# FFN up-projection as seven products per block pair (Strassen), with the second token half's norm behind products of the first

## The chip, the core and the metric

The kernel runs on one core of a Trainium2 chip. Its engines run beside one another, each through its own instructions in order: TensorE (PE) multiplies, and its weight loads (PEld) overlap its matmuls; VectorE (DVE), ScalarE (ACT) and GpSimd (POOL) work on elements; SyncE (SP) issues the transfers (DMAs). The metric is the device time of one execution in microseconds, the median of three runs.

## What is computed

One decoder layer over 16 meta tokens and 1024 tokens of width 1024, all in float32: retention and differential attention side by side, merged by gates, then a gated MLP with a causal convolution of three taps. Cut to the parts that the change touches:

```
do  = do @ w_diff_o                                   # 1024 x 1024
mix = (sigmoid(g_ret) * ro + sigmoid(g_diff) * do) @ w_out
h   = h + mix
u   = rmsnorm(h, norm2_w)
up  = causal_dwconv(u @ w_up, conv_w, conv_b)         # 1024 -> 2 x 2816
a, b = split(up)
h   = h + (silu(a) * b) @ w_down                      # 2816 -> 1024
```

## The kernel before

Activations lie transposed: channels on the 128 partitions in blocks, tokens along the columns. A float32 product is made of three matmuls of a shorter type: each operand is split into a high and a low part, and hi x hi, hi x lo and lo x hi are summed in PSUM. For weights this split is two instructions per [128, 4, 128] half block: ACT casts the high part (L227), POOL subtracts it from the raw weight for the low part (L230). The matmuls of all bulk products stand in one helper (L175).

The program runs through five stages. Phase 1 and phase 2 (projections, differential attention, retention and its output product, lines 942 and before) end near 1657 us. Phase 3 scales the eight attention heads (L971, split at L247), multiplies them by `w_diff_o` and merges them with the gates (L991 to L998), multiplies the result by `w_out` and adds it to the residual (`finish`, L1019), with the squares for the norm gathered on ACT and POOL (L1022 to L1026). Phase 4 is the FFN: for each of 22 blocks f of 128 hidden channels, `up(f)` and `up(22 + f)` multiply eight blocks of the input by one weight block over three token groups of 342 (two halo columns and 1024 tokens), so 8 x 3 x 3 = 72 matmuls. The input is h times the norm weight; the factor of the token, 1/rms, is multiplied onto the finished product (L1079), so that the products needn't wait for the norm. Then come the three taps of the convolution on DVE (`conv`, L1086 and L1088), Silu on ACT (L1124), the product with the other half (L1125), its split (ACT and POOL at L247), and for two blocks at a time the down product, 48 matmuls of 512 columns per block, added into h by DVE (L1103).

What sets the order: one list of weight blocks through the whole program (`self.stream`, `next_w`) keeps two blocks loaded and split ahead, from any stage into the next. Work for other engines that PE would wait for is put off by units of twelve matmuls (`defer`, `tick`). All tiles come from pools that live for the whole program.

## Time and profile before

| | us |
|---|---|
| median of three runs | 2614.26 (2612.69 to 2614.82) |
| profiled execution, first to last instruction (span) | 2609.7 |
| PE busy | 2520.9 (97%), 15444 matmuls |
| DVE busy | 1667.5 (64%) |
| ACT busy | 898.4 (34%) |
| POOL busy | 865.4 (33%) |

What lies outside the span of the profiled execution is the start and the end of the program, 4.6 us between the span and the median. A busy share is an average over the stages. What counts for a change in one stage is the table by windows: there each engine's busy time stands for one stretch, beside the clock that was granted to PE. A group of instructions gives the mean time of one; how close they follow one another is read from the starts in the timeline. The DMA queues of the page hold loads and stores that SP issues; none is issued from POOL.

### The profile page before, as it was taken

The numbers are of one execution on the slowest core, as the hardware profiler recorded it, in microseconds if no ns is written. First come the engines' busy times: TensorE is split into PE (matmuls) and PEld (weight loads), VectorE is DVE, ScalarE is ACT, GpSimd is POOL, SyncE is SP. The second block draws the span as 40 slices with busy tenths as digits, with TensorE's granted clock in tenths as the row PEclk, the third lists the DMA queues.
The fourth block names the chain that finished last, engine by engine and source line by source line (L and its number), as shares of the span: only waits on it lengthen the run. The fifth ranks groups of instructions, "written<-read, shape, count | busy, mean of one in ns | idle before, by whom it ended". The sixth has DMA issues, their size and how long they took to land.

```text
span 2609.7 us, 40439 instructions
## 1 busy us (share of the span) xinstructions
PE 2520.9 (97%) x15444; PEld 2420.4 (93%) x15444; DVE 1667.5 (64%) x3359; ACT 898.4 (34%) x1903; POOL 865.4 (33%) x644
## 2 busy tenths in 40 slices
PE   7899999999999999999999999999999999999999
PEld 6898999999999999999999898999999999999998
DVE  8687877657474756654677888452376555555555
ACT  3344434344252433433456654332321111111111
POOL 4433343313132222212333333443333333333332
PEclk8999999999999999999999999999999999999999
DMA  4121221222222121223343434523111111111112
GB/s 175 58 78 64 67 79 61 81 87 67 84 64 78 57 87 62 75 83 103 108 115 86 120 88 122 177 98 112 45 48 47 49 49 49 43 47 49 49 49 85
DMA packets 165777, 205.37 MB, mean 79 GB/s; under 512 B 25560, under 2 KB 108112, under 8 KB 165584
## 3 DMA queue, kind: packets, MB, share of 16 engines
q1 hardware_dynamic: 165440, 202.70, 24.4%
q8 instruction: 121, 1.98, 0.3%
q14 instruction: 72, 0.59, 0.1%
q10 hardware_dynamic: 144, 0.10, 0.0%
HBM read 160.20 MB, written 42.35 MB: 78 GB/s over the span
## 4 chain that ended last, share of the span: by engine, by line
PE 76%; DVE 15%; issue 4%; ACT 2%; DMA 2%; SPq 1%; POOL 0%; DVEq 0%; ACTq 0%; POOLq 0%
PE acc L175 43%; PE sc L175 27%; PE ot L175 3%; DVE b L567 3%; PE st L175 2%; DMA b<-d 1%; DVE b L499 1%; ACT b L609 1%; PE sc L625 1%; DVE b L602 1%; DVE al L247 1%; DVE b L501 1%; DVE sql L247 1%; DVE sh L498 1%; DVE b L521 1%
## 5 line engine op out<-in xcount | busy, mean ns | idle before, releaser
L175 PE MATMUL acc<-b,wh 128*128 128x342 f32 (+3 forms) x6076 | 1484.6, 327 | 30.7 <-DVE b L252 6.6
L175 PEld LDWEIGHTS acc<-b,wh 128*128 128x128 f32 x6076 | 1055.1, 190 | 46.3 <-DVE b L253 7.3
L175 PE MATMUL acc<-b,wl 128*128 128x342 f32 (+3 forms) x3038 | 987.2, 325 | 0.3 <-POOL wl L230 0.3
L230 POOL TENSOR_TENSOR wl<-wr,wh 128x512 fp32r<-128x512 f32 x370 | 514.1, 1408 | 1114.2 <-ACT wh L227 1103.8
L175 PE MATMUL sc<-b,wh 128*128 128x342 f32 (+2 forms) x2452 | 616.2, 334 | 0.0
L175 PEld LDWEIGHTS acc<-b,wl 128*128 128x128 f32 x3038 | 577.0, 190 | 5.7 <-POOL wl L230 0.6
L175 PEld LDWEIGHTS sc<-b,wh 128*128 128x128 f32 x2452 | 432.1, 189 | 20.9
L227 ACT CAST wh<-wr 128x512 fp32r<-128x512 f32 x370 | 214.6, 618 | 574.2 <-issue 286.3
L175 PE MATMUL sc<-b,wl 128*128 128x342 f32 (+2 forms) x1226 | 410.6, 335 | 0.8 <-POOL wl L230 0.8
L247 POOL TENSOR_TENSOR b<-b,b 128x512 fp32r<-128x512 f32 (+2 forms) x90 | 147.9, 1644 | 317.2 <-ACT b L242 275.4
L175 PEld LDWEIGHTS sc<-b,wl 128*128 128x128 f32 x1226 | 231.8, 189 | 11.4 <-POOL wl L230 1.3
L242 ACT CAST b<-b 128x512 fp32r<-128x512 f32 (+2 forms) x135 | 99.9, 745 | 233.0 <-DVE b L1125 146.2
L609 ACT ACTIVATE b<-b,sm 128x272 f32<-128x272 f32 (+7 forms) x128 | 100.9, 789 | 227.0 <-DVE sm L608 174.6
L534 DVE TENSOR_TENSOR ev<-acc,b 128x342 f32<-128x342 f32 (+1 forms) x144 | 74.0, 514 | 132.8 <-PE acc L175 115.8
L1088 DVE SCALAR_TENSOR_TENSOR b<-b,cols,b 128x1024 f32<-128x1024 f32 x88 | 148.8, 1691 | 2.3
L602 DVE CUSTOM_DVE_ANT_0 b<-sc,consts 128x144 f32<-128x144 f32 (+6 forms) x224 | 105.9, 503 | 42.7 <-PE sc L175 42.1
L1079 DVE TENSOR_TENSOR b<-sc,b 128x342 f32<-128x342 f32 x84 | 42.5, 511 | 137.3 <-PE sc L175 137.3
L247 DVE TENSOR_TENSOR al<-sc,ah 128x512 fp32r<-128x512 f32 (+2 forms) x144 | 77.5, 539 | 56.8 <-ACT ah L242 55.4
L1103 DVE TENSOR_TENSOR b<-b,sc 128x512 f32<-128x512 f32 x117 | 78.6, 682 | 48.9 <-PE sc L175 48.9
L242 ACT CAST ah<-sc 128x512 fp32r<-128x512 f32 (+2 forms) x144 | 67.3, 468 | 122.3 <-PE sc L625 94.5
L500 POOL TENSOR_TENSOR sh<-sh,b 128x346 f32<-128x346 f32 (+1 forms) x48 | 47.7, 994 | 153.4 <-DVE sh L498 125.5
L567 DVE TENSOR_TENSOR b<-b,b 64x346 fp32r<-64x346 f32 (+1 forms) x96 | 89.4, 931 | 3.7 <-ACT b L566 0.7
(230 smaller groups left out, 2849.6 us busy)
## 6 DMA issues: line engine op xcount, KB each, us to landing
wr<-w_in SPq DMA_DIRECT2D x176, 256.0 KB
wr<-w_up SPq DMA_DIRECT2D x88, 256.0 KB
d<-ev SPq DMA_DIRECT2D x120, 171.0 KB
b<-d SPq DMA_DIRECT2D x256, 64.0 KB
b<-d SPq DMA_DIRECT2D x24, 513.0 KB
wr<-w_down SPq DMA_DIRECT2D x44, 256.0 KB
b<-d SPq DMA_DIRECT2D x32, 260.0 KB
d<-ev SPq DMA_DIRECT2D x48, 173.0 KB
```

Of the source, the lines that this page charges most:

```text
L175: self.E.matmul(out, lhsT=l, rhs=r, start=start, stop=stop)
L227: self.A.copy(h, raw)
L230: self.G.tensor_sub(l, raw, h.bitcast(F32))
L242: self.A.copy(dh, src)
L247: (self.V if el == "V" else self.G).tensor_sub(dl, src, dh.bitcast(F32))
L500: G.tensor_mul(sh[:, :n], sh[:, :n], self.Sn[:, cs])
L534: V.tensor_mul(o[:, :n], ps[:, :n], self.rb[:, cs])
L567: V.tensor_sub(dst[o, cs], raw[r, cs], dst[r, cs].bitcast(F32))
L602: V.tensor_tensor_reduce(out=sc_[:m, a0:a0 + sz], in0=ps[:m, :sz], in1=mk, scale=1.0, scalar=3e38, op0=ALU.add, op1=ALU.min, accum_out=sm[ ...
L609: A.activation(sc_[:m, :n], sc_[:m, :n], AF.Exp, bias=mx, scale=-1.0, accum_out=sm[:m, 10 + c:11 + c])
L1088: V.scalar_tensor_tensor(out=o[:, q], in0=up[:, NMETA - 2 + i:T - 2 + i], scalar=self.cw(i, fi), in1=o[:, q], op0=ALU.mult, op1=ALU.add)
L1103: self.V.tensor_add(h, h, ps)
```

## The change

**The up-projection.** For a pair of weight blocks (f and 22 + f), the input channels are cut in two halves, the tokens in two halves of 516 columns (two pieces of 258), and the two blocks are the two halves of the output. That is a 2 x 2 matrix product, and it is made with seven products instead of eight, by Strassen's algorithm in Winograd's form. The products are named A, B, D, E, F, G, H. A and B use plain quarters of the input; E, F, G, H use sums and differences of its quarters, made once (`operand_e` to `operand_h`); each product has 4 x 3 x 2 = 24 matmuls of 258 columns. Their weights are sums of quarters too, made for each pair: two of the sums by DMAs that add what they load to what lies in SBUF, issued from POOL (`quad_sums`, L1291 and L1292), two by POOL (`weights`, names S and T, L1303 and L1305); every weight quarter is then cast by ACT and split by POOL (L983). B, H, G and D are accumulated onto the bank of an earlier product after DVE or ACT has read that bank, so that a bank holds running sums. DVE has five reads of PSUM per pair (L1417, L1427, L1434, L1439, L1442), ACT two. The first tap of the convolution goes from DVE to ACT (`Identity` with a scale and a bias); the other two are on DVE as before, in halves of 512 columns (L1340), put between the reads of the next pair, the product with the other half too (L1356).

**Norm.** Sums of halves of the tokens need inputs with the norm's factor in them. So h is multiplied by 1/rms and the norm weight before the products (`scaled`, L1238). w_out is done in two token halves, and its weights are loaded twice; the norm of the first half runs during the second half's products, that of the second half behind the products A and B of the first three pairs, which need the first half alone.

**Order.** The pools of phases 1 and 2 are closed and others opened (`back`), with their own weight queue, quarter tiles (11 for high and low parts, 8 raw) and PSUM layout; the last two blocks of `w_ret_o` are moved behind that border. Head norms are put between the products of the merge, one at a time (`normed_head`). The results of all 22 pairs are stored to DRAM, and all down products come after the last pair, with the same number of matmuls as before; h waits in DRAM meanwhile.

```diff
+    def back(self, ctx):
...
+        self.flush()
+        self.front.close()
+        tc, a = self.tc, self.a
+        pool = lambda n, b=1, **k: ctx.enter_context(tc.tile_pool(name=n, bufs=b, **k))
+        self.tp = pool("tmp2", 1)
+        self.wp = pool("w2", 11)
+        self.ps = pool("ps2", 3, space=PSUM)
+        self.queue = [a["w_ret_o"][14], a["w_ret_o"][15]] + [a["w_diff_o"][i] for i in range(8)] + 2 * [a["w_out"][i] for i in range(8)]
...
+    HALF = [[(12, 256), (268, 256)], [(524, 258), (782, 258)]]
+    PIECES = [(0, 258), (258, 258)]
...
+        for i, pieces in enumerate(self.HALF):
+            x = lambda k: (mh[k], ml[k])
+            outs = lambda ps: [(ps[:, 512 * g:512 * g + 512], t0, n) for g, (t0, n) in enumerate(pieces)]
...
+    def operand_e(self):
+        for k in range(4):
+            self.scaled(k, 1)
+            self.V.tensor_sub(self.half(k, 0), self.half(k, 0), self.half(k, 1))
+            self.put("E", k, self.half(k, 0), "G" if k % 2 else "V")
...
+    def operand_f(self):
+        for k in range(4):
+            self.scaled(4 + k, 1)
+            self.V.tensor_add(self.half(k, 0), self.half(4 + k, 1), self.half(k, 0))
+            self.put("F", k, self.half(k, 0), "G" if k % 2 else "V")
...
+    def operand_g(self):
+        for k in range(4):
+            self.V.tensor_sub(self.half(4 + k, 0), self.half(4 + k, 0), self.half(k, 0))
...
+    def operand_h(self):
+        for k in range(4):
+            self.V.tensor_sub(self.half(k, 1), self.half(k, 1), self.half(4 + k, 1))
...
+        blk, blk2 = self.a["w_up"][f], self.a["w_up"][NF + f]
+        lo, hi = slice(0, 4), slice(4, 8)
+        s1, s3 = self.raw_quarter(blk2[:, lo, :]), self.raw_quarter(blk2[:, lo, :])
+        ra = self.raw_quarter(blk[:, lo, :])
+        rb = self.raw_quarter(blk[:, hi, :])
+        rd = self.raw_quarter(blk2[:, hi, :])
+        self.raws[f] = dict(a=ra, b=rb, d=rd, s1=s1, s3=s3)
...
+    def quad_sums(self, f):
+        r = self.raws[f]
+        self.nc.gpsimd.dma_start(out=r["s1"], in_=self.a["w_up"][NF + f][:, 4:, :], accum_op=ALU.add)
+        self.nc.gpsimd.dma_start(out=r["s3"], in_=self.a["w_up"][f][:, :4, :], accum_op=ALU.add)
...
+            if n == "S":
+                self.G.tensor_add(r["a"], r["a"], r["s1"])
+            elif n == "T":
+                self.G.tensor_add(r["b"], r["b"], r["a"])
+            else:
+                q[n] = self.split_w(r[dict(A="a", B="b", F="a", H="s3", E="s1", G="d", D="b")[n]])
...
+    def quad_product(self, ps, f, name, more=False):
+        w = self.wq[f].pop(name)
+        outs = [(ps[:, 512 * g:512 * g + 512], t0, n) for g, (t0, n) in enumerate(self.PIECES)]
+        self.product(outs, [((w[0][:, k, :], w[1][:, k, :]), self.xs(name, k)) for k in range(4)], not more, True, more)
...
         for f in range(NF):
+            todo = {1: ["F", "H", "G", "TD"], 2: ["SE", "F", "H", "G", "TD"]}.get(f + 1, ["A", "SF", "B", "H", "E", "TG", "D"])
...
+                pt = self.dbl()
+                self.quad_product(pt, f, "A")
+                A.copy(bd(ua[:, 516:1032]), self.pair(pt, 258))
+                others()
...
+            self.quad_product(pw, f, "F")
+            V.tensor_sub(bd(sw), bd(st), self.pair(pw, 258))
+            others()
+            if f >= self.PRO:
+                self.quad_product(pt, f, "B", True)
+                A.copy(bd(ua[:, :516]), self.pair(pt, 258))
+                others()
...
+            self.quad_product(pw, f, "H", True)
+            V.tensor_sub(bd(su), self.pair(pw, 258), bd(st))
+            others()
...
+                self.quad_product(pv, f, "E")
+            V.tensor_sub(bd(ub[:, 516:1032]), bd(su), self.pair(pv, 258))
...
+            self.quad_product(pw, f, "G", True)
+            V.tensor_sub(bd(ub[:, :516]), self.pair(pw, 258), bd(st))
+            others()
+            self.quad_product(pv, f, "D", True)
+            V.tensor_add(bd(ua[:, 516:1032]), bd(sw), self.pair(pv, 258))
```

How the instructions stand at three places. Names: `wr` is a raw weight, `wh` and `wl` its parts, `b` a large SBUF tile, `d` a PSUM tile of the new layout, or in a DMA a DRAM tile, `sw`, `su` kept sums.

SP at the end of phase 2, before: loads of heads (L967, L970) with weights of the stream between.

```order
L221 DMA wr_18334<-w_ret_o 128x512
L221 DMA wr_18424<-w_ret_o 128x512
L967 DMA b_18658<-d_7050 128x1026
L970 DMA b_18659<-d_7051 128x258
L970 DMA b_18659<-d_7051 128x256 x3
L967 DMA b_18670<-d_8607 128x1026
L221 DMA wr_18428<-w_ret_o 128x512
L221 DMA wr_18518<-w_diff_o 128x512
```

SP at the same place after: heads (L1039, L1042), then the first weights of the back.

```order
L1042 DMA b_18797<-d_8611 128x256 x3
L1039 DMA b_18826<-d_10167 128x1026
L1042 DMA b_18827<-d_10168 128x258
L1042 DMA b_18827<-d_10168 128x256 x3
L977 DMA wr_18443<-w_ret_o 128x512
L977 DMA wr_18445<-w_ret_o 128x512
L977 DMA wr_18455<-w_ret_o 128x512
L977 DMA wr_18457<-w_ret_o 128x512
L977 DMA wr_18571<-w_diff_o 128x512
```

The weight loads of `w_ret_o` stood between loads of the heads and ran on into `w_diff_o`; now those of the last two blocks stand together behind the border.

DVE at the start of the FFN, before: the end of the norm's chain, then the first products multiplied by its result (L1119) and their taps.

```order
L280 TENSOR_TENSOR sq_20435<-sq_20435,ry_20434 128x342
L283 SCALAR_TENSOR_TENSOR ry_20434<-sq_20435,ry_20434 128x342
L253 SCALAR_TENSOR_TENSOR ryl_20446<-ry_20434,ryh_20445 128x342
L1119 TENSOR_TENSOR b_20551<-acc_20366,b_20345 128x342
L1119 TENSOR_TENSOR b_20551<-sc_20367,b_20345 128x342
L1119 TENSOR_TENSOR b_20551<-sc_20368,b_20345 128x342
L1086 TENSOR_SCALAR b_20555<-b_20551,cols 128x1024
L1119 TENSOR_TENSOR b_20559<-sc_20369,b_20345 128x342
L1088 SCALAR_TENSOR_TENSOR b_20555<-b_20551,cols,b_20555 128x1024
L1119 TENSOR_TENSOR b_20559<-sc_20370,b_20345 128x342
```

DVE at the start of the FFN after: the end of the operands' sums (31 instructions from the first L1238 to the last L1260), then the first read of a product F (L1417).

```order
L250 TENSOR_TENSOR b_21010<-b_19528,b_21009 128x516
L1265 TENSOR_TENSOR b_19530<-b_19530,b_19538 128x516
L1265 TENSOR_TENSOR b_19532<-b_19532,b_19540 128x516
L1265 TENSOR_TENSOR b_19534<-b_19534,b_19542 128x516
L1260 TENSOR_TENSOR b_19536<-b_19536,b_19528 128x516
L250 TENSOR_TENSOR b_21012<-b_19532,b_21011 128x516
L1260 TENSOR_TENSOR b_19538<-b_19538,b_19530 128x516
L250 TENSOR_TENSOR b_21030<-b_19536,b_21029 128x516
L1260 TENSOR_TENSOR b_19540<-b_19540,b_19532 128x516
L1260 TENSOR_TENSOR b_19542<-b_19542,b_19534 128x516
L1417 TENSOR_TENSOR sw_21061<-u_20695,d_21064 128x516
L250 TENSOR_TENSOR b_21032<-b_19540,b_21031 128x516
```

The read of F, for which the bank of H waits, stands behind the sums of all of E, F, H and G.

POOL in the middle of the FFN, before: from the split of one block's activation (L247) to the next, low parts of weights (L230) of two up and two down blocks.

```order
L247 TENSOR_TENSOR b_23082<-b_22982,b_23081 128x1024
L230 TENSOR_TENSOR wl_23160<-wr_23161,wh_23159 128x512
L230 TENSOR_TENSOR wl_23160<-wr_23165,wh_23159 128x512
L230 TENSOR_TENSOR wl_23234<-wr_23235,wh_23233 128x512
L230 TENSOR_TENSOR wl_23234<-wr_23239,wh_23233 128x512
L230 TENSOR_TENSOR wl_23327<-wr_23328,wh_23326 128x512
L230 TENSOR_TENSOR wl_23327<-wr_23332,wh_23326 128x512
L230 TENSOR_TENSOR wl_23426<-wr_23427,wh_23425 128x512
L230 TENSOR_TENSOR wl_23426<-wr_23431,wh_23425 128x512
L247 TENSOR_TENSOR b_23422<-b_23322,b_23421 128x1024
```

POOL in the middle of the FFN after, one pair: low parts (L983), sums (L1303, L1305) and the accumulating DMAs for the pair after (L1291, L1292).

```order
L983 TENSOR_TENSOR wl_22548<-wr_22438,wh_22547 128x512
L1303 TENSOR_TENSOR wr_22438<-wr_22438,wr_22434 128x512
L983 TENSOR_TENSOR wl_22586<-wr_22438,wh_22585 128x512
L983 TENSOR_TENSOR wl_22617<-wr_22440,wh_22616 128x512
L1305 TENSOR_TENSOR wr_22440<-wr_22440,wr_22438 128x512
L983 TENSOR_TENSOR wl_22648<-wr_22436,wh_22647 128x512
L983 TENSOR_TENSOR wl_22691<-wr_22434,wh_22690 128x512
L1291 DMA wr_22920<-w_up 128x512
L983 TENSOR_TENSOR wl_22725<-wr_22442,wh_22724 128x512
L983 TENSOR_TENSOR wl_22754<-wr_22440,wh_22753 128x512
L1292 DMA wr_22922<-w_up 128x512
```

Per pair of up blocks there are nine operations and two DMA issues; before, there were four for up, two for down on average, and the activation's.

DVE beside it, after, one pair:

```order
L1340 SCALAR_TENSOR_TENSOR b_24245<-b_24011,cols,b_24245 128x512 x2
L1417 TENSOR_TENSOR sw_24252<-b_24217,d_24255 128x516
L1340 SCALAR_TENSOR_TENSOR b_24245<-b_24011,cols,b_24245 128x512 x2
L1340 SCALAR_TENSOR_TENSOR b_24244<-b_23974,cols,b_24244 128x512 x4
L1427 TENSOR_TENSOR su_24253<-d_24255,b_24217 128x516
L1356 TENSOR_TENSOR b_24244<-b_24244,b_24245 128x512 x2
L1434 TENSOR_TENSOR b_24254<-su_24253,d_24352 128x516
L1439 TENSOR_TENSOR b_24254<-d_24255,b_24217 128x516
L1442 TENSOR_TENSOR b_24217<-sw_24252,d_24352 128x516
```

Six taps (two and four at L1340) stand between the reads of F (L1417) and H (L1427).

## Rows read from the trace of the kernel before

**Rows 1.** The page's head: span, busy time by engine, granted clock in 40 slices.
```profile
span 2609.7 us, 40439 instructions
...
PE 2520.9 (97%) x15444; PEld 2420.4 (93%) x15444; DVE 1667.5 (64%) x3359; ACT 898.4 (34%) x1903; POOL 865.4 (33%) x644
...
PEclk8999999999999999999999999999999999999999
```

**Rows 2.** Windows: busy us (instructions) of each engine, clock, DMA; first line names columns.
```profile
core 0: us, PE busy (x) PEld busy (x) DVE busy (x) ACT busy (x) POOL busy (x), PEclk, DMA share, GB/s
1600.00:1650.00 50.00, 43.43 (x257) 41.02 (x256) 36.77 (x85) 16.12 (x35) 15.34 (x10) 0.97 0.42 135
1650.00:1700.00 50.00, 46.92 (x298) 46.56 (x297) 22.01 (x29) 18.99 (x22) 27.09 (x15) 1.00 0.55 189
...
1900.00:2000.00 100.00, 100.00 (x591) 95.62 (x591) 62.31 (x62) 17.67 (x26) 36.09 (x23) 1.00 0.15 48
...
1606.00:1612.00 6.00, 5.51 (x21) 4.95 (x22) 5.04 (x20) 2.03 (x3) 0.62 (x1) 0.72 0.12 44
```

**Rows 3.** Groups, PE, 1590 to 1665: shapes, count, busy, mean, idle before, releasers.
```profile
L175 PE MATMUL acc<-b,wh 128*128 128x342 f32 x212 | 51.5, 326 | 8.3 <-DVE b L942 5.2 <-DVE b L247 1.7 <-ACT b L242 1.4
```

**Rows 4.** Chain that ended last, 1616 to 1656: start us, us, what.
```profile
1620.19 3.22 DMA b<-d
...
1646.12 5.65 DMA b<-d
```

**Rows 5.** Timeline of PE, 698.9 to 702.2: start us, us, what, how many.
```profile
699.04 0.28 PE L175 MATMUL ot<-ah,vh 128*128 128x256 f32 x1
699.16 0.28 PE L175 MATMUL ot<-al,vh 128*128 128x256 f32 x1
699.27 0.28 PE L175 MATMUL ot<-ah,vl 128*128 128x256 f32 x1
699.39 0.22 PE L175 MATMUL ot<-ah,vh 128*128 128x128 f32 x1
...
700.68 0.47 PE L175 MATMUL acc<-b,wh 128*128 128x342 f32 x2
...
701.62 0.66 PE L175 MATMUL sc<-b,b 128*128 128x264 f32 x4
702.11 0.32 PE L175 MATMUL acc<-b,wh 128*128 128x342 f32 x1
```

**Rows 6.** Timeline of PE, 2003 to 2009.
```profile
2003.07 0.63 PE L175 MATMUL sc<-b,wh 128*128 128x512 f32 x2
...
2008.39 0.39 PE L175 MATMUL sc<-b,wl 128*128 128x512 f32 x1
```

**Rows 7.** Timeline of POOL, 1849 to 1864, DVE idle beside it.
```profile
1850.35 2.54 POOL L230 TENSOR_TENSOR wl<-wr,wh 128x512 fp32r<-128x512 f32 x2 [2.22 <-ACT wh L227]
```

**Rows 8.** Groups, ACT, 1660 to 2600.
```profile
L227 ACT CAST wh<-wr 128x512 fp32r<-128x512 f32 x164 | 93.9, 618 | 385.6 <-issue 191.9 <-PE sc L175 108.8 <-PE acc L175 81.4
L1124 ACT ACTIVATE b<-b 128x1024 f32<-128x1024 f32 x22 | 23.3, 1061 | 108.1 <-DVE b L1088 108.1
```

**Rows 9.** Groups, DVE, 1700 to 2600.
```profile
L1088 DVE SCALAR_TENSOR_TENSOR b<-b,cols,b 128x1024 f32<-128x1024 f32 x88 | 148.8, 1691 | 2.3
...
L1103 DVE TENSOR_TENSOR b<-b,sc 128x512 f32<-128x512 f32 x114 | 76.5, 682 | 46.8 <-PE sc L175 46.8
...
L283 DVE SCALAR_TENSOR_TENSOR ry<-sq,ry 128x342 f32<-128x342 f32 x2 | 1.0, 516 | 0.1
```

**Rows 10.** Timeline of DVE, 2071 to 2073, POOL idle beside it.
```profile
2071.66 1.27 DVE L1088 SCALAR_TENSOR_TENSOR b<-b,cols,b 128x1024 f32<-128x1024 f32 x1
```

**Rows 11.** Timeline, 2044 to 2050, DVE and POOL.
```profile
2044.45 1.87 DVE L1086 TENSOR_SCALAR b<-b,cols 128x1024 f32<-128x1024 f32 x1
2044.48 3.00 POOL L230 TENSOR_TENSOR wl<-wr,wh 128x512 fp32r<-128x512 f32 x2 [8.30 <-ACT wh L227]
...
2046.35 3.52 DVE L1088 SCALAR_TENSOR_TENSOR b<-b,cols,b 128x1024 f32<-128x1024 f32 x2
```

**Rows 12.** One line's instructions, 1580 to 1700: issues of weight loads (ns min/median/max).
```profile
L221 SPq DMA_DIRECT2D wr<-w_diff_o x9: 332/333/371, 1644.3 to 1697.6; - x9
```

**Rows 13.** Groups, POOL, 1660 to 2600.
```profile
L230 POOL TENSOR_TENSOR wl<-wr,wh 128x512 fp32r<-128x512 f32 x164 | 233.9, 1448 | 444.7 <-ACT wh L227 444.7
L247 POOL TENSOR_TENSOR b<-b,b 128x1024 fp32r<-128x1024 f32 x22 | 53.2, 2419 | 119.6 <-ACT b L242 119.6
```

## Prediction before the run

> **What bounds the kernel now.** First the page's head [rows 1]: TensorE (PE) is busy 97% of the span at a granted clock of full speed in nearly every slice, the next engine, DVE, 64%, POOL 33%. An average hides stages, so next the table by windows [rows 2]: in the FFN, which is the last 740 us, PE is busy 100.00 of 100 us, at granted clock 1.00 (the 2.4 GHz level), with DVE at 62 and POOL at 36. There the time is the number of matmuls times their spacing, nothing else. Only one stretch behind the start is open: 1600 to 1700, with 6.6 and 3.1 us of idle PE, where the accumulators of the retention output wait for DVE, which is itself stuck behind the head norms written ahead of them [rows 3]; the chain there runs through loads of 3.2 and 5.7 us [rows 4]. After the idle the clock falls: 0.72 in 1606 to 1612 [rows 2], that is a part of it at the 1.2 GHz level.
>
> So a change that takes columns from the FFN is paid in full, as long as the other engines keep up with the shorter stream.
>
> **PE's stream.** Spacing is read from starts of neighbours. 342 columns: 6 matmuls from 700.68 to 701.62, 157 ns each; 264 columns: 4 in 0.49 us, 122 ns; 256 columns, with a weight tile of its own each: 3 from 699.04 to 699.39, 117 ns [rows 5]; 512 columns: 23 from 2003.07 to 2008.39, 231 ns [rows 6]. A line through them gives 120 ns for 258 columns. The up-projection is now 44 blocks of 8x3x3 = 72 matmuls: 3168 x 157 ns = 497 us. Strassen's form has, for each of 22 pairs, 7 products of 4x3x2 = 24 matmuls of 258 columns: 3696 x 120 ns = 443.5 us. Gain 54 us; a product lasts 2.88 us and a pair 20.2 us. w_out in token halves: 576 x 157 = 90.4 us become 768 x 119.5 = 91.8 us, +1. The down products are 1056 of 512 columns in both. Stream: **-53 us**.
>
> **What is added beside it, per pair of the FFN.** POOL: 7 low parts and 2 weight sums of 128x512. Two such operations alone take 2.54 us [rows 7], so 1.29 each with a little overlap, 11.6 us, and two accumulating DMAs. ACT: 7 casts of 0.62, 4 taps, two copies and a Silu of 1.06 [rows 8], some 9 us: free. DVE: 5 evacuations of 516 columns (0.68 at 512, one input in PSUM [rows 9]) 3.5 us, and 8 taps and 2 multiplications of 512 with both inputs in SBUF. 1024 columns of that take 1.27 us undisturbed [rows 10] and 342 take 0.52 [rows 9], so 0.7 for 512: 7 us, together 10.5 of 20.2. By busy time all fits. But DVE operations with two SBUF inputs and POOL exclude one another here: in 2044 to 2050 two POOL operations take 3.00 instead of 2.54, and two taps 3.52 where two undisturbed ones take 2.5; what POOL still had to do when they began, to 2047.5, is simply added to them [rows 7, 10, 11]. In the trace the mean tap is 1691 ns [rows 9]. So count POOL and these DVE operations as one resource: 11.6 + 7.0 = 18.6 us, and twice the POOL time of an accumulating DMA. The trace of before has no DMA issued from POOL. Bounds: 0.33 us, an issue on SP's queue [rows 12], and 2.42 us, POOL's longest plain operation [rows 13]; I take 0.8, nearer the issue, since the engine has only to start the transfer. Sum 20.2 (19.3 to 23.4) against PE's 20.2: level.
>
> The Trainium skill, "SBUF — State Buffer", section "Who interferes with whom", says it as a rule: a DVE instruction with two SBUF inputs contends with a GpSimd instruction that reads SBUF, and one with one SBUF input does not. The trace agrees for the taps. Without the rule, with separate engines, POOL would stand at 13 of 20.2 us and this term would be zero.
>
> Where does that reach PE? A bank is reused one product after the product that filled it, so F must be evacuated before H, H before G, E before D, each with 2.88 us of cover. In DVE's order six taps stand between the evacuations of F and H. From F's evacuation done (about 6.5 us into the pair) to the last moment for H (13.7) there are 7.2 us; six taps are 4.2, and POOL, paced by PE's release of weight tiles (one per product), puts some 3.2 operations, 4.1 us, in between: 8.3. So 0 (POOL happens to run elsewhere) to 1.1 us per pair, in 19 pairs 0 to 21 us; I take **+10**. The landing of the accumulating DMAs has no part in it: they are issued a pair ahead of their reader on POOL, three or four operations before it.
>
> **The start of the FFN, second token half.** In before the norm factor is applied behind the product, so nothing waits (100% PE). Now the sums E, F, G, H need normed data. Behind the last w_out product stand 6 products that need only the first half, 17.3 us of PE. The norm chain (add, square, add, cast, low part, sums, 9 small DVE operations of some 0.4 to 0.5, split, spread, copy) has to wait for its place on PE behind five of them, 14.4 us, and ends near 16.2. Then DVE has 31 operations of 516 columns, all with two SBUF inputs, ahead of the evacuation of the first F: 31 x 0.7 + 0.7 = 22.4 us, to 38.6. PE has E, E and F in that time and would stand before the first H at 26.4 without a stall. So 12 us of idle PE as the lower bound. On top POOL has in the same time some 8 low parts of operands and up to 9 weight operations, of which up to 11 (14 us) can fall between DVE's: 26 us as the upper bound. Most of the weight work can be done before the norm is ready, so I take **+15**, clock drops after the idle included.
>
> **The border of front and back.** The back has its own pools, opened when the front's are closed: the first back weight load waits for the last front matmul, and with it the prefetch across stages is gone. Issue 0.33 [rows 12], landing 3.2 to 5.7 (the loads of [rows 4]), cast 0.62 [rows 8]: 4.2 to 6.7 us, of which nothing is covered; **+5**. The idle of 1600 to 1700 goes in part: head norms are now spread between products, evacuations come ahead of them. Of 9.7 us [rows 2] between 2 and 9.7 go; **-6**.
>
> **w_out's second half.** POOL has there some 13 low parts of weights, 6 for the first FFN weights, 4 for operands and 7 square sums, 30 x 1.29 = 39 us, DVE some 20 operations of two SBUF inputs, 13 us: 52 in 46 us. Two blocks are prefetched, 5 us of POOL. Between 0 and 8 us, **+3**. The end (last adds and stores) is as before.
>
> **Sum.** -53 + 10 + 15 + 5 - 6 + 3 = -26 on the profiled 2609.7: 2583.7. The profiled span is 4.6 us below the median of the runs, 2614.26; with it 2588.
>
> **Rivals.** (a) *The shared POOL/DVE resource sets the pair.* For it: the sum is level at the middle estimate and a queue in order has no slack to lose. Against: POOL may run up to four products ahead, and taps and evacuations are placed apart. It decides from an issue of about 1.9 us: then a pair takes 18.6 + 3.8 = 22.4 us, 2.2 over PE's, x 19 = 42 us in place of 10: 2620, slower from there on. At the bound of 2.42 a pair is 23.4: 3.3 x 19 = 62, time 2640. That is the case with the other sign.
>
> The Trainium skill, same page, section "A bandwidth-pool intuition that's wrong (but worth ruling out)", has a rule against this change: a GpSimd DMA of 620 ns took 3100 ns under a DVE copy, since its descriptors need the port. With 3.1 us the pair would be 24.8 us and the time, as an estimate, some 2665. The same page limits it to DVE's two-port modes (copy, cast, tensor_scalar) and infers that two-input operations leave the write side free; the steady state has none of these on DVE. No row here shows either, so it moves the chance of (a) only a little.
>
> (b) *The starts eat the gain*: the start of the FFN at 26, border 7, w_out 8, pairs at 21, idle saved 2: -53 + 60 = +7, time 2621 at the very worst; with two or three of them at their bound 2600 to 2612, no change that matters. (c) *All cover holds*: pairs 0, w_out 0, start 12, border 4, idle saved 9.7: -47, time 2568. (d) *258 columns do not run at 120 ns in long rows*, because each matmul brings a weight tile: only runs of three or four neighbours show it. At 133 ns the gain of 54 is gone over 4464 matmuls; at the bound of 157 (no faster than 342) the time is about 2750. The groups of three in [rows 5] speak against it.
>
> **Chances.** Forecast (2570 to 2608) 0.62; (a) 0.16; (b) 0.11, half of it within 0.2%; (c) 0.07; (d) 0.04. A measurement of this kernel tells about 0.2%, 5 us, from no change. Faster: 0.62 + 0.07 + a third of (b) = 0.72; same 0.08; slower 0.20. The range goes from (c) less a few us for a start better than counted, 2562, to between the threshold and the bound of (a), 2628.
>
> **What will show it.** Right: rows of 120 ns for 258 columns in the profile after; windows of the FFN's up part with PE at 97% or more, some 20.5 us per pair; one idle stretch of 10 to 20 us in front of the first H, released by DVE; a gap of 4 to 7 us at the border, ended by ACT or a DMA. Wrong: PE waiting in every pair for POOL's low parts (case a, POOL's queue full and its DMA issues long), for DVE's evacuation of F or H by more than 1 us, or spacings above 130 ns (case d).

## The result, and the profile after

The changed kernel takes 2628.18 us (median of 4 runs, 2626.38 to 2631.42), the kernel before 2613.96 beside it: a ratio of 1.0054 [1.0040, 1.0069], so **slower by 0.5%**, 14 us. The forecast was 26 us faster; the result has the other sign and lies 0.2 us past the upper end of the range, less than the runs scatter. (Of e4, below, one run of two counts; the other took 13644 us.)

The page's head, which answers to [rows 1]:

```profile
span 2625.3 us, 42939 instructions
...
PE 2491.9 (95%) x16168; PEld 2384.5 (91%) x16168; DVE 1674.7 (64%) x3332; ACT 1041.2 (40%) x2132; POOL 1088.4 (41%) x833
...
PEclk8899999999999999999999999999889999999999
```

PE is busy 29 us less than before, and the span is 15.6 us longer: the work went down and idle time came. In the last third of PEclk are two slices that were not there in [rows 1]. The shorter stream itself is as forecast. In the timeline of PE near 2100 (start, duration, what, how many):

```profile
2100.32 0.65 PE L1016 MATMUL d<-b,wh 128*128 128x258 f32 x4
2100.80 0.40 PE L1016 MATMUL d<-b,wl 128*128 128x258 f32 x2
2101.04 0.64 PE L1016 MATMUL d<-b,wh 128*128 128x258 f32 x4
```

From 2100.32 to 2101.04 six matmuls of 258 columns start, 120 ns each. Where the time went, by windows, with the columns of [rows 2]:

```profile
1850.00:1900.00 50.00, 39.78 (x307) 38.77 (x306) 25.03 (x25) 17.14 (x33) 39.70 (x32) 0.92 0.49 125
1900.00:1950.00 50.00, 32.09 (x204) 30.71 (x205) 40.94 (x44) 20.75 (x33) 32.79 (x23) 0.74 0.19 47
2000.00:2100.00 100.00, 97.14 (x796) 95.92 (x795) 66.30 (x70) 39.84 (x63) 64.18 (x52) 1.00 0.43 112
2350.00:2400.00 50.00, 46.58 (x269) 40.83 (x268) 32.70 (x34) 20.61 (x29) 26.98 (x16) 0.93 0.70 241
```

Three places are open: the second half of w_out with the start of the FFN (1850 to 1950), every pair behind it, and the start of the down products (2350 to 2400). A busy share doesn't show what a low clock costs, so the rest of this text goes by PE's **loss** in a stretch: the time from the first matmul's start to the last one's, less what the same matmuls take at 120 ns (258 columns), 157 (342) and 231 (512). It was 46.0 us in w_out's second half with the start of the FFN, up to the end of the fourth pair; 15.7 from the fifth pair to the last (pairs 4 to 21 in the expectations, which count from 0); 6.6 at the start of the down products. In all three it was under 1 us before.

What PE waited for in 1860 to 1960 (us in total, times, longest), then in 1980 to 2340:

```profile
PE d L1016 <- DVE sw L1417: 9.3, 2, 8.0
PE s L178 <- ACT b L245: 5.0, 1, 5.0
PE d L1016 <- POOL b L250: 4.2, 2, 2.9
PE d L1016 <- DVE b L250: 3.6, 1, 3.6
...
PE d L1016 <- DVE su L1427: 4.9, 7, 1.0
PE d L1016 <- DVE b L1434: 4.7, 9, 1.1
```

The forecast single gap before the first H is there, 8.0 us behind DVE's read of F (L1417), but it is less than half of the waits: the norm's column sums (`s`, L178) and the operands E and F (L250) stop PE before it. After such waits PE runs slower: the granted clock of 1900 to 1950 is 0.74, a part of it at the 1.2 GHz level. In PE's timeline:

```profile
1904.20 1.06 PE L1016 MATMUL d<-b,wh 128*128 128x258 f32 x4
1905.06 0.63 PE L1016 MATMUL d<-b,wl 128*128 128x258 f32 x2
```

Four matmuls in 0.86 us, 215 ns each in place of 120. Between 1868 and 1962 that is 7.7 us of the loss, the waits (read from the starts of neighbours) 31.7.

DVE's timeline over the same stretch, in brackets the idle time before a row and who ended it; then POOL's:

```profile
1868.17 0.69 DVE L1130 TENSOR_TENSOR b<-b,d 128x516 f32<-128x516 f32 x1 [5.09 <-PE d L1016]
1876.49 1.74 DVE L1138 TENSOR_TENSOR b<-b,su 128x516 f32<-128x516 f32 x1 [7.63 <-POOL b L1138]
...
1894.11 1.43 DVE L1238 SCALAR_TENSOR_TENSOR b<-b,cols,b 128x516 f32<-128x516 f32 x2 [4.71 <-ACT b L1165]
1895.45 4.66 DVE L1249 TENSOR_TENSOR b<-b 128x516 f32<-128x516 f32 x2
...
1916.86 4.77 DVE L1265 TENSOR_TENSOR b<-b,b 128x516 f32<-128x516 f32 x3
...
1928.43 0.68 DVE L1417 TENSOR_TENSOR sw<-u,d 128x516 f32<-128x516 f32 x1
```

```profile
1862.22 0.88 POOL L1291 DMA_DIRECT2D wr<-w_up  x1 [2.34 <-DMA wr<-w_up]
...
1875.19 1.27 POOL L1138 TENSOR_TENSOR b<-b,sw 128x516 f32<-128x516 f32 x1
...
1886.26 1.41 POOL L1303 TENSOR_TENSOR wr<-wr,wr 128x512 f32<-128x512 f32 x1 [2.68 <-DMA wr<-w_up]
```

The last residual is added at 1868.2, the first operand begins at 1894.1, F is read at 1928.4. The norm took 25.2 us from the end of the last add (the forecast 16.2 from the last product): its last sum of squares on POOL (1875.19) stood behind weight work, and that behind accumulating DMAs, for which POOL waited until a plain load of weights had landed (2.34 us at 1862). The wait of 2.68 at 1886 comes after that sum; weight work stands behind it. The row of operands took 34.3 us (forecast 22.4).

The groups of 1990 to 2330, to set against [rows 9]:

```profile
L1340 DVE SCALAR_TENSOR_TENSOR b<-b,cols,b 128x512 f32<-128x512 f32 x128 | 140.1, 1150 | 61.8 <-ACT b L1336 61.8
...
L1292 POOL DMA_DIRECT2D wr<-w_up x15 | 13.3, 888 | 42.8 <-DMA wr<-w_up 23.7 <-PE d L1016 19.1
L1291 POOL DMA_DIRECT2D wr<-w_up x15 | 13.3, 887 | 54.1 <-DMA wr<-w_up 50.4 <-PE d L1016 3.8
...
L1417 DVE TENSOR_TENSOR sw<-b,d 128x516 f32<-128x516 f32 x16 | 10.9, 681 | 0.0
```

The issue of an accumulating DMA costs POOL 0.89 us (taken: 0.8), but POOL stood idle in front of them for 96.9 us in 15 pairs, 6.5 a pair, 74.1 us of it until a raw load had landed. DVE stood idle before its taps for 61.8 us, waiting for the first tap on ACT (L1336). A tap, with both inputs in SBUF, took 1150 ns on average beside POOL; the read of F, with one input in PSUM, took 681.

The start of the down products, in PE's timeline, and ACT's behind it:

```profile
2368.71 0.73 PE L1016 MATMUL d<-b,wh 128*128 128x512 f32 x2 [1.52 <-ACT b L245]
2371.35 1.22 PE L1016 MATMUL d<-b,wh 128*128 128x512 f32 x2 [1.91 <-POOL b L250]
```

```profile
2367.03 0.62 ACT L982 CAST wh<-wr 128x512 fp32r<-128x512 f32 x1 [2.27 <-PE d L1016]
2367.61 1.04 ACT L245 CAST b<-b 128x1024 fp32r<-128x1024 f32 x1
```

The cast of the first reloaded activation (L245) stands behind a cast of a weight (L982) whose tile PE has to give back.

### The profile page after: what moved, and what is told of

The parts are those of the page before. It is cut to its first block, busy times and chain, and to the rows that moved or that the text cites. A ratio compares the mean times of both kernels' runs of the same rounds, so it can differ in the third digit from the quotient of the medians.

```text
span 2625.3 us, 42939 instructions
## 1 busy us (share of the span) xinstructions
PE 2491.9 (95%) x16168; PEld 2384.5 (91%) x16168; DVE 1674.7 (64%) x3332; ACT 1041.2 (40%) x2132; POOL 1088.4 (41%) x833
## 5 line engine op out<-in xcount | busy, mean ns | idle before, releaser
L178 PE MATMUL acc<-b,wh 128*128 128x342 f32 (+2 forms) x4784 | 1163.1, 326 | 25.3 <-ACT wh L230 6.0
L178 PEld LDWEIGHTS acc<-b,wh 128*128 128x128 f32 x4784 | 829.0, 191 | 29.8 <-ACT wh L230 6.0
L1016 PE MATMUL d<-b,wh 128*128 128x258 f32 (+3 forms) x4000 | 759.3, 309 | 39.6 <-DVE sw L1417 9.3
L178 PE MATMUL acc<-b,wl 128*128 128x342 f32 (+2 forms) x2392 | 771.8, 323 | 0.0
L1016 PEld LDWEIGHTS d<-b,wh 128*128 128x128 f32 x4000 | 604.8, 192 | 77.4 <-DVE sw L1417 10.1
L178 PEld LDWEIGHTS acc<-b,wl 128*128 128x128 f32 x2392 | 455.0, 190 | 0.1
L1016 PE MATMUL d<-b,wl 128*128 128x258 f32 (+3 forms) x2000 | 451.8, 307 | 0.0
L983 POOL TENSOR_TENSOR wl<-wr,wh 128x512 fp32r<-128x512 f32 x250 | 343.7, 1402 | 193.5 <-ACT wh L982 180.3
L1016 PEld LDWEIGHTS d<-b,wl 128*128 128x128 f32 x2000 | 329.5, 192 | 15.5
L982 ACT CAST wh<-wr 128x512 fp32r<-128x512 f32 x250 | 151.5, 618 | 359.8 <-PE d L1016 215.4
L250 POOL TENSOR_TENSOR b<-b,b 128x512 fp32r<-128x512 f32 (+4 forms) x109 | 181.5, 1672 | 218.6 <-ACT b L245 181.9
L1340 DVE SCALAR_TENSOR_TENSOR b<-b,cols,b 128x512 f32<-128x512 f32 x164 | 172.8, 1105 | 82.3 <-ACT b L1336 82.2
L230 ACT CAST wh<-wr 128x512 fp32r<-128x512 f32 x202 | 118.5, 619 | 185.4 <-issue 95.6
L245 ACT CAST b<-b 128x512 fp32r<-128x512 f32 (+4 forms) x164 | 116.6, 721 | 173.7 <-DMA b<-d 67.3
L245 ACT CAST ah<-sc 128x512 fp32r<-128x512 f32 (+2 forms) x144 | 67.3, 468 | 122.2 <-PE sc L628 96.0
L250 DVE TENSOR_TENSOR al<-sc,ah 128x512 fp32r<-128x512 f32 (+2 forms) x144 | 77.5, 538 | 55.8 <-ACT ah L245 54.5
```

The lines of the kernel that those rows point to most:

```text
L178: self.E.matmul(out, lhsT=l, rhs=r, start=start, stop=stop)
L230: self.A.copy(h, raw)
L245: self.A.copy(dh, src)
L250: (self.V if el == "V" else self.G).tensor_sub(dl, src, dh.bitcast(F32))
L982: self.A.copy(w[0], raw)
L983: self.G.tensor_sub(w[1], raw, w[0].bitcast(F32))
```

## The experiments

Ratios are to the kernel before, with 95% intervals. "Start" is the loss in w_out's second half with the start of the FFN, "pairs" that of the fifth pair to the last, "down" that at the start of the down products. e2, e4, e7 and e9 leave out a part of the result; the others compute the whole layer.

| kernel | us | ratio | start | pairs | down |
|---|---|---|---|---|---|
| after | 2628.2 | 1.0054 [1.0040, 1.0069] | 46.0 | 15.7 | 6.6 |
| e1 first tap ahead | 2619.2 | 1.0014 [1.0005, 1.0024] | 43.4 | 7.7 | 6.4 |
| e2 no accumulating DMAs | 2601.3 | 0.9949 [0.9930, 0.9969] | 34.4 | 1.7 | 6.0 |
| e3 squares on DVE | 2620.4 | 1.0024 [1.0012, 1.0035] | 39.3 | 16.1 | 6.6 |
| e4 low parts on ACT, later pairs | 2612.0 (one run) | | 43.6 | 1.7 | 6.6 |
| e5 early raw loads | 2626.6 | 1.0043 [1.0028, 1.0058] | 48.9 | 11.7 | 5.8 |
| e6 F read first | 2632.1 | 1.0062 [1.0045, 1.0079] | 50.5 | 16.0 | 6.2 |
| e7 no second norm | 2623.9 | 1.0035 [1.0021, 1.0048] | 42.7 | 15.3 | 6.4 |
| e8 e1, e3, e5, e6, loads | 2619.4 | 1.0015 [1.0006, 1.0025] | 44.9 | 5.5 | 5.9 |
| e9 low parts on ACT, start | 2609.7 | 0.9981 [0.9971, 0.9991] | 26.9 | 15.0 | 6.8 |
| e10 a fourth pair as cover | 2641.7 | 1.0106 [1.0091, 1.0122] | 60.2 | 15.1 | 6.6 |
| e11 e1, e3, loads | 2610.6 | 0.9986 [0.9977, 0.9995] | 38.6 | 6.3 | 6.8 |
| e12 e11 and e10 | 2634.0 | 1.0077 [1.0060, 1.0094] | 60.7 | 7.4 | 6.4 |
| e13 e11, operands on DVE | 2613.6 | 0.9993 [0.9984, 1.0003] | 41.8 | 6.1 | 5.4 |
| e14 e11, down load early | 2607.1 | 0.9969 [0.9956, 0.9982] | 37.3 | 8.3 | 0.9 |
| e15 e11, less cover | 2615.5 | 1.0005 [0.9995, 1.0014] | 43.6 | 6.8 | 5.7 |
| e16 e13, e14, e15 | 2611.8 | 0.9990 [0.9981, 1.0000] | 40.8 | 6.7 | 0.8 |

### The pairs: e1, e2, e4, e5

e1 changes one order on ACT: the first `Identity` tap of a pair comes ahead of the copy of A.

```diff
+        yield
         taps(ob, NF + f, ub, hv[0])
...
             act = self.act_steps(f, ua, ub)
+            next(act)
```

> One edit: the activations that begin the convolution's taps of the second half block are issued on ACT before the copy of the next pair's product A, not behind it. Theory 'ACT order': in the changed kernel DVE stands idle 3.9 us in each pair until this activation comes (it waits on ACT behind the copy of A), so its six taps begin 3 us late and the read of F or H comes 0.4 to 1 us after PE wants the bank. With the activation earlier the loss of PE in the pairs falls from 18 us to under 6, and the time by some 12 us, to about 2616. Rival 'POOL and DVE exclude one another': the taps are slow because of POOL, wherever they begin; the loss stays above 14 us and the time falls by 4 us at most.

Half of the pairs' loss goes, 15.7 to 7.7, and 9 us of the time; that lies between the two forecasts. So one part of it is plain order. But more than ACT's order changed in the kernel as it ran. DVE's timeline of e1, from the read of F (L1418) to that of H (L1428):

```profile
2142.14 0.68 DVE L1418 TENSOR_TENSOR sw<-b,d 128x516 f32<-128x516 f32 x1
2142.74 1.84 DVE L1340 SCALAR_TENSOR_TENSOR b<-b,cols,b 128x512 f32<-128x512 f32 x2
2145.70 1.29 DVE L1357 TENSOR_TENSOR b<-b,b 128x512 f32<-128x512 f32 x2 [1.12 <-ACT b L1354]
2146.92 0.69 DVE L1428 TENSOR_TENSOR su<-d,b 128x516 f32<-128x516 f32 x1
```

Between the reads of F and H stand two taps and the two multiplications, where the changed kernel has six taps; the other taps are spread over the rest of the pair. POOL's idle time in front of its DMA issues in 1990 to 2330 fell too, from 96.9 to 38.9 us. The copy, the bunch of six taps and POOL's waits are not told apart by e1.

e2:

```diff
-        self.nc.gpsimd.dma_start(out=r["s1"], in_=self.a["w_up"][NF + f][:, 4:, :], accum_op=ALU.add)
-        self.nc.gpsimd.dma_start(out=r["s3"], in_=self.a["w_up"][f][:, :4, :], accum_op=ALU.add)
```

> The two accumulating DMAs of each pair are left out (the weight sums lack these parts). Theory 'waits in POOL's queue': they cost PE little in the pairs, where the low parts are made in time (loss there 18 us, plus or minus 3), but at the start of the FFN POOL stands idle at them for raw weights to land (2.3, 1.1, 1.1, 2.7 and 2.2 us), with the sums of squares queued behind; without them the loss from 1826 to 1960 falls from 43 to about 33 us. Rival 'the accumulating DMAs set the pair' (case a of the prediction): the loss in the pairs falls under 8 us.

My theory said 18 us would stay in the pairs, and 1.7 stayed: here it fell, and the rival was right. What it said of the start held: 46.0 to 34.4. Traffic fell as well, a DMA share of 0.27 in place of 0.43 in 2000 to 2100, and no run sets that apart. The issues themselves are 2 x 0.89 a pair; POOL's idle time in front of them, 6.5 a pair, is what I take to push POOL's other nine operations together into the time of the taps. PE and POOL of e2 in the window of 2000 to 2100, columns as above:

```profile
2000.00:2100.00 100.00, 100.00 (x832) 100.00 (x832) 64.89 (x75) 44.30 (x70) 62.66 (x45) 1.00 0.27 91
```

PE has no idle time, with POOL nearly as busy as in the kernel after (62.7 and 64.2).

e4 takes low parts of weights off POOL from the fifth pair on:

```diff
+        if act:
+            self.A.copy(w[1], raw)
+        else:
+            self.G.tensor_sub(w[1], raw, w[0].bitcast(F32))
...
-                q[n] = self.split_w(r[...])
+                q[n] = self.split_w(r[...], f > 3)
```

> From the fifth pair on the low parts of the up weights are not subtracted by POOL; ACT writes a second cast in their place (the low parts are left out of the result). POOL then has the two sums and two DMA issues per pair. Theory 'exclusion': a tap of 512 columns falls from 1.1 us (mean in the changed kernel) to 0.7, the reads of F and H are in time, the loss in the pairs falls from 18 to under 6 us. Theory 'ACT order': the taps are shorter but still begin 3 us late, and ACT has 4.3 us more per pair in front of them: the loss stays above 10 us.

The taps' group in 1990 to 2330, of e1 and then of e4:

```profile
L1340 DVE SCALAR_TENSOR_TENSOR b<-b,cols,b 128x512 f32<-128x512 f32 x136 | 145.2, 1083 | 89.2 <-ACT b L1336 87.9
```

```profile
L1343 DVE SCALAR_TENSOR_TENSOR b<-b,cols,b 128x512 f32<-128x512 f32 x136 | 93.8, 748 | 65.5 <-ACT b L1339 65.5
```

With POOL out of the way a tap takes 748 ns, with it 1083 to 1150, and with POOL gone the loss goes with it. But in e1 the tap is nearly as slow as in the kernel after, and half of the loss is gone, and e4 keeps the accumulating DMAs: taking away any one of the order, POOL's waits and POOL's work undoes much of the term. None of them is its only cause.

e5 issues the raw loads of the next pair but one at the start of a pair, with a ninth raw tile:

```diff
+            if f + 2 < NF and f:
+                self.quad_loads(f + 2)
...
             V.tensor_sub(bd(ub[:, 516:1032]), bd(su), self.pair(pv, 258))
-            if f + 2 < NF and f:
-                self.quad_loads(f + 2)
```

> The raw weights of the pair after next are loaded at the start of a pair, not behind its product E, into nine raw tiles, not eight. Everything else as in the changed kernel. Theory 'POOL waits at the accumulating DMA': their issue is short (0.89 us each in the trace), but POOL stands idle in front of them until the raw weights they add to have landed: 54 and 43 us in 15 pairs, so that its low parts are pressed together with the taps. With the loads earlier this idle time falls under 35 us together and the loss of PE in pairs 4 to 21 from 15.7 to under 6 us, time about 2618. Rival 'the issues themselves are in the way': idle time falls, the loss stays above 12 us.

POOL's idle time before the issues fell from 96.9 to 41.4 us (32.4 and 9.0), and the pairs' loss by 4; what was saved there came back in part at the start (48.9). Neither forecast is met (idle under 35 with a loss under 6, or a loss above 12). The wait goes with the landing of the load, but one more tile is not enough to take it away.

### The start: e3, e7, e6, e9, e10

e3 moves the second half's sums of squares from POOL to DVE:

```diff
-                (V if i and m == 7 else G).tensor_add(sq[:, hs], sq[:, hs], x)
+                (V if i else G).tensor_add(sq[:, hs], sq[:, hs], x)
```

> One edit: the sums of squares of the second token half are made by DVE instead of POOL. Theory 'waits in POOL's queue': the norm's chain at the end of w_out starts 5 to 7 us late, because POOL's last sum of squares stands behind weight work and waits for loads; on DVE it is made at once, PE's waits of 5.2 and 2.5 us at the sums over channels go, the loss from 1826 to 1960 falls from 43 to about 36 us, time about 2621. Rival 'exclusion': the chain is as long as before since DVE's additions with two SBUF inputs wait for POOL all the same: 43 plus or minus 2, time unchanged.

As expected: the loss fell by 6.7 us. The norm took 15.6 us in place of 25.2, near the 16.2 forecast, so its excess was the wait for POOL's queue. But the row of operands grew from 34.3 to 39.5 and took part of that back.

e7 takes the statistics of the second half out and uses the first half's factor:

```diff
                         spread(0)
+                        spread(1)
...
-        squares(1)
...
-            if f == 1:
-                stat()
...
-        spread(1)
```

> The norm of the second token half is left out: its tokens are scaled with the first half's factors, so that nothing has to wait for squares, sums over channels and reciprocal roots at the start of the FFN; the operands are built as before. Theory 'the norm's chain is what lacks cover': the operands can begin some 25 us earlier, beside the products A and B, and the loss from w_out's second half to pair 4 falls from 46.0 to 12 to 18 us. Rival 'building the operands on DVE against POOL sets it': 31 operations take 34 us in the changed kernel, and the loss stays above 30 us.

Only 3.3 us, less than with e3. PE then stood 15.6 us for DVE's add of w_out's products (L1130), 11.0 of it at once. This doesn't isolate the norm: the second half's operands now stand among those adds on DVE, from 1855 to 1907, and the read of F at 1919.9 waited 12.7 us for PE. So e7 says little of the norm alone; with the operands' work beside w_out's products PE loses about as much (42.7 us) as with it behind them.

e6 reads F ahead of the sums of H, G and D:

```diff
             V.tensor_sub(bd(sw), bd(st), self.pair(pw, 258))
+            if f == 0:
+                self.weights(0, "H")
+                self.operand_h()
+                self.weights(0, "G")
+                self.operand_g()
...
```

> At the start of the FFN the read of the first product F is written ahead of the sums for the operands H, G and D. Prediction's step: the bank of H waits for that read behind 31 operations of DVE. With six to seven of these behind it, PE's wait in front of the first H falls from 8.3 to 2 to 4 us, the loss from w_out's second half to pair 4 from 46.0 to about 40 us, time about 2622. Rival 'H waits for its operand anyway': 46 plus or minus 1.5, time unchanged.

The wait in front of the first H went to 1.8 us, and the next one came in its place. PE's waits in 1860 to 1965 of e6:

```profile
PE d L1016 <- DVE su L1428: 10.4, 1, 10.4
...
PE d L1016 <- DVE sw L1410: 3.3, 2, 1.8
```

e9 writes the low parts of the first four pairs' weights on ACT (the edit of e4, with `f < 4`, and in `pre_weights`):

> For the first four pairs the low parts of the up weights are not subtracted by POOL; ACT writes a second cast in their place (these low parts are left out of the result). POOL keeps the sums, the DMA issues, the squares and its low parts of operands. Theory 'at the start too, DVE and POOL exclude one another, and the weight work of POOL is what lengthens DVE's row': the 31 operations from the first scaling to the last sum fall from 34 us to 23 to 26, and the loss from w_out's second half to pair 4 from 46.0 to 25 to 32 us. Rival 'DVE's row and the norm's chain are as long by themselves': the loss stays above 40 us.

DVE's timeline, from the first operand to the read of F:

```profile
1886.38 1.43 DVE L1241 SCALAR_TENSOR_TENSOR b<-b,cols,b 128x516 f32<-128x516 f32 x2 [4.26 <-ACT b L1168]
...
1914.66 0.68 DVE L1420 TENSOR_TENSOR sw<-u,d 128x516 f32<-128x516 f32 x1
```

28.3 us in place of 34.3, and the loss 26.9 in place of 46.0: the largest step that any edit made at the start. The row was expected shorter still (23 to 26); half of the operands' low parts are on POOL in this kernel too. The norm got shorter as well, 15.7 us in place of 25.2, with those low parts gone from POOL's queue. So of the 15.5 us by which F is read earlier after the last residual, 9.5 are the norm's wait and 6.0 the row.

What lengthens the row can be counted in the traces. Of its 31 operations in the changed kernel 21 took under 0.78 us and ten took longer, 13.7 us more together; each of the ten overlaps an operation of POOL. Operations of POOL that begin inside the row, without issues of DMAs, against what DVE's longer operations had over 0.685 us:

| kernel | POOL operations | DVE us over | row |
|---|---|---|---|
| e9 | 7 | 7.6 | 28.3 |
| after | 12 | 13.7 | 34.3 |
| e11 | 16 | 19.9 | 38.9 |
| e3 | 17 | 20.4 | 39.5 |
| e10 | 22 | 26.1 | 49.2 |

That is 1.1 to 1.2 us of DVE's time for each operation of POOL, which alone takes 1.29. The reads with one input in PSUM are the other side: all 104 of them behind 1900 us in the changed kernel took 675 to 697 ns.

e10 computes A and B of a fourth pair in the cover (`PRO = 4`, with the weights for it, `pre_weights(3)`, and `first_t(3)`, `first_b(3)` behind `first_b(2)`):

```diff
-    PRO = 3
+    PRO = 4
...
         self.first_b(2)
+        self.first_t(3)
+        self.first_b(3)
```

> Four pairs, not three, have their products A and B made before the products that need the second token half: 5.8 us more of PE's work as cover. Theory 'cover is short': the loss from w_out's second half to pair 4 falls from 46.0 to about 40, the time by 5 us, to about 2622. Rival 'the shared work of DVE and POOL is the measure': the two low parts and casts of that pair come into the same stretch, and the loss is 45 to 48.

5.8 us more for PE to do in the cover, and 14 us more loss. DVE's timeline, then POOL's, then PE's:

```profile
1932.89 9.26 DVE L250 TENSOR_TENSOR b<-b,b 128x516 fp32r<-128x516 f32 x1
1942.06 0.68 DVE L1420 TENSOR_TENSOR sw<-u,d 128x516 f32<-128x516 f32 x1
```

```profile
1932.96 5.25 POOL L250 TENSOR_TENSOR b<-b,b 128x516 fp32r<-128x516 f32 x4
1937.87 1.18 POOL L1295 DMA_DIRECT2D wr<-w_up  x1
1938.48 3.10 POOL L250 TENSOR_TENSOR b<-b,b 128x516 fp32r<-128x516 f32 x2
```

```profile
1942.89 1.20 PE L1016 MATMUL d<-b,wh 128*128 128x258 f32 x4 [19.59 <-DVE sw L1420]
```

The loss, 60.2, is far above both forecasts. One DVE operation, which takes 0.68 alone, is busy for 9.26 us, as long as POOL has six operations of 1.3 and an issue in a row. It stands right ahead of the read of F, for which PE has been waiting.

### Together: e8, e11, e12

e11 has the edits of e1 and e3, and both down loads ahead of the first split:

```diff
+        xs = [self.big() for _ in range(2)]
+        for i in range(2):
+            self.S.dma_start(out=xs[i][:, :SEQ], in_=self.acts[2 * p + i])
         for i in range(2):
-            x = self.big()
-            self.S.dma_start(out=x[:, :SEQ], in_=self.acts[2 * p + i])
+            x = xs[i]
```

e8 is e11 with e5 and e6, e12 is e11 with e10.

> Four edits together: the taps' first activation ahead of the copy of A, squares of the second half on DVE, raw weights loaded earlier with nine tiles, the read of the first F ahead of the sums; beside them both stored activations of a down step are loaded before the first is split. If the causes are separate: loss in pairs 4 to 21 under 5 us (15.7 in the changed kernel), from w_out's second half to pair 4 about 31 (46.0), start of the down products 3 (6.6): time about 2597, 0.6% below the kernel before. If one of them only moves the wait to the next one: 2605 or more.

> The two edits that each took PE's waits away, together: the taps' first activation ahead of the copy of A, and the second half's squares on DVE; beside them both stored activations of a down step are loaded before the first is split. If they are separate: loss in pairs 4 to 21 near 7.7, from w_out's second half to pair 4 near 38, start of the down products 4 to 6; time about 2612, within 0.2% of the kernel before. If the start answers to the new order as in the combined run before (44.9): about 2617.

> The run before with the fourth pair's A and B as cover as well. If cover is short: loss from w_out's second half to pair 4 about 33, time about 2607, 0.3% below the kernel before. If shared work of DVE and POOL is the measure: 38 to 40, time about 2613.

The two orders of e11 bring 18 us and turn the sign; its losses are near those expected if the two are separate. What e6 and e10 did alone they did in company as well: e8 (2619) falls under its second forecast, 2605 or more, and e12 (2634) is above both of its own. The start of the down products hardly moved in any of them.

### What was left: e13 to e16

e13 puts all operands' low parts on DVE, e14 calls `down_load(0)` ahead of the last pair's loads of `w_down`, e15 takes the second pair's weight sum S and product E out of the cover, e16 does all three, each on top of e11:

```diff
-            self.put("E", k, self.half(k, 0), "G" if k % 2 else "V")
+            self.put("E", k, self.half(k, 0), "V")
...
+                down = self.down_load(0)
...
-        self.weights(1, "SE")
...
-        for f in range(2):
+        for f in range(1):
```

> On top of the kernel of e11, the low parts of all operands E, F, G, H of the second token half on DVE (in e11 half of them, 8, are on POOL). Theory: the start is set by POOL's and DVE's work with two SBUF inputs added together, and DVE loses more than the work itself where POOL has several operations queued; 8 operations of POOL at 1.3 us become 8 of DVE at 0.7, so the loss of w_out's second half and the start falls from 38.6 to 31 to 34 us, time about 2605. Rival: DVE's own row of operations sets it; then 8 x 0.7 us are added, and the loss is 40 to 44, time 2612 to 2616.

The loss rose, by as much as the rival said, but not as it said. DVE's row got shorter (1884.67 to 1920.34, 35.7 us; in e11 38.9), and POOL's next low part paid. DVE's timeline, then POOL's:

```profile
1914.28 0.69 DVE L1260 TENSOR_TENSOR b<-b,b 128x516 f32<-128x516 f32 x1
1914.88 1.90 DVE L250 TENSOR_TENSOR b<-b,b 128x516 fp32r<-128x516 f32 x3
1916.70 1.90 DVE L1260 TENSOR_TENSOR b<-b,b 128x516 f32<-128x516 f32 x3
1918.52 1.90 DVE L250 TENSOR_TENSOR b<-b,b 128x516 fp32r<-128x516 f32 x3
...
1928.69 6.71 DVE L1340 SCALAR_TENSOR_TENSOR b<-b,cols,b 128x512 f32<-128x512 f32 x2 [0.94 <-ACT b L1336]
```

```profile
1913.29 8.26 POOL L983 TENSOR_TENSOR wl<-wr,wh 128x512 fp32r<-128x512 f32 x1 [2.14 <-ACT wh L982]
```

It is the mirror of e10: here DVE runs at 0.61 us an operation, and POOL's, 1.29 alone, is busy for 8.26. What POOL had left then fell on DVE's first taps, 6.71 us for two, and PE waited 2.9 us for the read of G behind them and 1.9 for a read two pairs later.

> On top of the kernel of e11, the reload of the first activations for the down-projection stands ahead of the last pair's loads of w_down in the queues, and its casts ahead of their casts on ACT. Theory: the 6.6 us at the start of the down-projection are ACT's cast of the reloaded activation standing behind casts of weight tiles that PE has yet to free; the loss there falls to 3 us or less, time 2606 to 2608, all else as in e11. Rival: it is the landing of the reload or the two low parts on POOL after it that come last; then 5 to 7 us stay, time 2610 to 2611.

The loss at the start of down is 0.9 us and the time inside the theory's band; the start's loss is 1.3 lower than in e11 and the pairs' 2.0 higher, though nothing there was edited. ACT's timeline of e14 shows the cast well ahead of its use, and the window (columns as above) PE at full clock with 1.0 us idle in place of 3.4:

```profile
2335.56 1.05 ACT L245 CAST b<-b 128x1024 fp32r<-128x1024 f32 x1 [0.39 <-DMA b<-d]
```

```profile
2350.00:2400.00 50.00, 48.97 (x231) 40.16 (x230) 33.97 (x30) 22.46 (x28) 40.16 (x21) 1.00 0.69 242
```

> On top of the kernel of e11, the second pair's first weight sum and its product E are taken out of the cover of the norm and stand in the second pair as in every other. Theory: POOL has 4 weight operations fewer in the stretch before the first H (low parts and sum, some 4 us), PE one covering product fewer (2.9 us); where POOL's and DVE's work sets the start, both nearly cancel: loss 37 to 40 us, time 2609 to 2612. Rival: the cover sets it, the weight work does not; then 2.9 us and more are lost: 41 to 44 us, time 2613 to 2616. If POOL's queue costs DVE more than its own time, the loss falls below 36.

The loss is in the rival's band, so the cover counts. Of the weight work it says nothing: POOL had 24 instructions in 1885 to 1930, and 25 in e11, so the list behind moved up into the gap.

> The edits of e13, e14 and e15 together on top of the kernel of e11. Theory: the effects add, loss of the start 31 to 35 us, of the start of down 3 or less, time 2600 to 2604, 0.4 to 0.5% below the kernel before. Rival: what is saved at the start is taken up by the next wait in DVE's row (as when F was read first); then only the start of down gains: 2606 to 2609.

Of the losses only the gain of e14 stays, and the time, 2611.8 with runs from 2606.8 to 2618.4, is above both forecasts and not below e11's. **e14 is the fastest version that computes the layer**: 2607.1 us, 0.3% below the kernel before.

## Why the prediction was wrong, point by point

- **PE's stream, -53: right.** 120 ns at 258 columns; rival (d) did not happen.
- **Border, +5, and old idle, -6: right in mechanism, small in size.** At the border PE lost 5.2 us, 3.4 of it behind ACT's first cast of a back weight. Of the 12.4 us lost in 1600 to 1652 before, 9.2 stayed, so -3 in place of -6: PE's waits for DVE's norm (L942, then L939) fell from 5.2 us to 2.1, one for ACT further up grew from 1.3 to 2.7.
- **w_out's second half, +3: right in size, by luck.** It lost 3.8 us up to the last residual, but PE waited there only once, 1.5 us for ACT's cast in the first half's norm (L253), and most of the rest is low clock behind that wait. That POOL's and DVE's shared work, from which the term was made, is behind it no run shows.
- **The pairs, +10 with bounds 0 to 21: inside the bounds, above the value.** 15.7 from the fifth pair on, some 0.9 a pair. The resource that DVE and POOL share was named, the issue well guessed, and the place too: PE waits for the reads that stand behind the six taps (L1427, L1434). But the sum of a pair was not what decides: e2 has nearly the same sum and no loss. What I missed was what the order of ACT and DVE costs (e1: 8.0 of the 15.7) and that POOL waits, with all that is queued behind, until the load has landed to which an accumulating DMA adds (e2, without these DMAs: 14.0; the two overlap). I had written that the landing has no part in it; that holds for the DMA's own reader, not for the load that it adds to.
- **The start of the FFN, +15 with bounds 12 to 26: the step that failed.** The loss from the last residual to the end of the fourth pair was some 42 us. Two links were too short. The norm took 25.2 us in place of 16.2, since I let POOL's square sums run when they were ready and not when POOL's queue came to them; e3, which takes them out of that queue, has 15.6. The row took 34.3 in place of 22.4: its 31 operations were priced alone, and POOL's share between them left to a bound of 11 operations, 14 us, of which the +15 holds 3, with the reason "Most of the weight work can be done before the norm is ready". Twelve operations of POOL fell into the row and cost 13.7: seven low parts of operands and five of weights, before which POOL had stood 2.18 us for a load and 3.66 for ACT's cast. Together the two links are 21 us. Low clock (7.7 us of the loss) was put inside the +15 without a price, and the earlier waits, for E's and F's operands, were not seen at all.
- **The start of the down products, 0: wrong**, 6.6. I had costed the same number of matmuls, not the reload in front of them, whose cast stands in ACT's queue behind weights for which PE has no free tile. e14 shows it.
- **Sum.** -53 + 2 (border, old idle) + 46 + 16 + 7 = +18; the profiled spans differ by +15.6. The missing 2 us are not placed.
- **The rivals.** (b), the starts eat the gain, is what happened, and beyond its own worst case of 2621. (a) was right in part: without POOL's accumulating DMAs the pairs lose nearly nothing (e2), but through the wait in front of them and not an issue of 1.9 us, and with them the loss goes too when POOL has less else to do (e4).
- **What contends.** That a DVE operation with one SBUF input doesn't contend with POOL was read too widely. It holds for the reads of PSUM, but in the kernel before the first tap (L1086, one SBUF input) took 0.81 us once, when POOL was idle, and 1.87 in 41 of its 44 times, all beside POOL.

The Trainium skill, "SBUF — State Buffer", section "Summary: rules for kernel authors", says that of a DVE operation with two SBUF inputs and a GpSimd operation that reads SBUF, the second to issue fully blocks until the first finishes. That one of the two stands still agrees with the rows of e10 and e13. The length doesn't: the waits of 9.26 (e10) and 8.26 us (e13) outlast six and more operations of the other engine, so the blocked engine did not get in after the first of them. Which of the two issued first the rows don't tell; in e10 DVE's begins 0.07 us ahead of POOL's.

What stays open: how much of the start's 37 us in e14 could be got back. The row's excess over 31 operations alone is POOL's work beside it, by the count above, but what PE would wait for next without it no run shows: e9 took 19 us off and shortened norm and row at once, and the attempts that keep the computation (e13, e15, e16) moved the work and gained nothing there.

## What to carry to other kernels

The gain in columns on the engine that bounds the stage came in full here; what ate it were the joints, where an operand is built that was free before. Cost each joint as a row in each engine's queue, with what that queue still has ahead, not as a chain of ready times; add to a row of DVE operations with two SBUF inputs nearly the whole time of each POOL operation that can fall into it; and look for instructions that nobody waits for ahead of ones that somebody does (the copy of A, the weight casts ahead of the reload): moving them brought 9 us (e1, where DVE's order moved too) and 3.5 (e14 against e11) here.

## What the runs showed of the hardware

- POOL and DVE with two SBUF inputs didn't take turns where one had its queue full: 0.68 became 9.26 us for DVE (e10), 1.29 became 8.26 for POOL (e13). Over a row, each operation of POOL cost DVE 1.1 to 1.2 us (after, e3, e9, e10, e11), while reads of PSUM beside POOL kept their 0.68.
- An accumulating DMA of 256 KB took 0.89 us of POOL for the issue and 4.1 us to its landing. Its price was neither of these, but POOL's wait in front of it, 6.5 us a pair, three quarters of it until a raw load had landed.
- More cover made the start slower (e10): 22 operations of POOL fell into the row in place of 12. I take this to come from the work on weights for the added pair, which stands in POOL's queue ahead of the operands; no run sets it apart.
